# First token tile of a flow-matching step: three z blocks multiplied in float32 while the modulation columns arrive in pairs, modulation as columns with stationary weights

## The chip, the core and the metric

The kernel runs on one core of a Trainium2 chip. The metric is device time in microseconds (us) for one execution. Three runs of the kernel before gave 2206.56, 2209.3 and 2211.78 us (median 2209.3). One execution was recorded by the hardware profiler; its span, from the first to the last instruction, is 2205.0 us.

The engines are named as in the profile: PE multiplies matrices, PEld is its weight load (one operand of a product is loaded and stays put, "stationary", while the other "moves" through), DVE, ACT and POOL work on vectors, and SP issues most of the loads and stores.

## The reference, cut to what matters

One layer for two groups of tokens, 2048 sample tokens and 128 prompt tokens, each of 1024 numbers. Only the head of it is touched here:

```python
def ada_mod(cvec, w, b):
    m = jnp.einsum('...d,de->...e', jax.nn.silu(cvec), w) + b
    return jnp.split(m, 3, axis=-1)

shift, scale, gate = ada_mod(c, w_ada[l], b_ada[l])
xn = rmsnorm(h, ln_g[l]) * (1.0 + scale[:, None, :]) + shift[:, None, :]
...
proj = jnp.einsum('btd,de->bte', xn, w_in)
qkv, beta, dec, z_a, u_b, v_b, z_b, x_c, z_c, gates = jnp.split(proj, points, axis=-1)
...
o = rmsnorm(o, o_norm_g) * jax.nn.silu(z_a.astype(jnp.float32).reshape(B, T, H_A, DV))
```

So a vector product with `w_ada` (1024 x 2048 of it is used here, 8.4 MB) gives a shift and a scale for each of the 1024 channels, the normalised tokens are modulated with them, and then multiplied by the columns of `w_in`. The four blocks of 128 columns called z (`z_a`, silu of the product) come first.

## The kernel before, in words

**The shape of the work.** A channel index of 1024 is eight rows of 128 partitions, `k` = 0..7 (`KT` = 8). Tokens are cut into tiles `TBS`: four of 512 and one of 128. Products with `w_in` are made in three float16 parts: a weight block is split into `hi` and `lo`, the modulated tokens into `xh` and `xl`, and for each `k` there are three products, hi·xh, hi·xl, lo·xh (`gemm_T`, all recorded under L161, where the helper `mm` stands). To split without overflow, one scale `sx` for all tokens is taken from a bound on the modulation (L425 to L430).

**The modulation.** L396 to L415 run over eight blocks of 256 columns of `w_ada`; blocks 0 to 3 are shift, 4 to 7 are scale. Each block comes in two loads `ast` of 512 KB (L403, `ast` has 8 buffers). The products have the two condition columns `scT` stationary and the weights moving: eight products of 256 columns in float32 for a block. In blocks 0, 2, 4 and 6 (`AD`) the second half is instead summed on DVE (`ada_sum`, L384 and L386) and added through two products with `sel`. The result is a row, copied (L413) and turned into columns by small products with the identity (L415), all eight blocks into the one bank `pa`. The first token tile is loaded ahead of block 4 (`XB`).

**What follows it.** When the last block is in, L420 to L422 make `sh` and `ms` for all eight `k`, then come the bound and `sx`. Four z weights are fetched (`getw(4)` with two `wst` buffers, so that the third and fourth load when the first two have been split) and converted to `zhi` and `zlo` (L209, L222, L223).

**The tile loop** (L442 to L472) does for each of the five tiles: squares of the tokens on ACT (L451), the reciprocal root (L170 on DVE, L171 on POOL), scaling on DVE (L455), transposing on PE (L459; 128 x 128 pieces, 32 for a tile of 512), modulating into `xm` on DVE (L461), `xh` on ACT (L462), `xl` on POOL (L463), then four z blocks of 24 products, each with a sigmoid on ACT (L468), a gating product on DVE (L469) and a store (L471).

**What sets the order.** The program is written once, and a scheduler puts the instructions of each engine into one fixed sequence. An engine executes its own sequence in order: an instruction that waits holds up all behind it on that engine, loads on SP as well. A load into a buffer waits until the last reader of that buffer is done. Behind the tile loop the z results are used much later; the q, k and v blocks of `w_in` follow at once.

## Time and profile before

| what | value |
|---|---|
| three runs | 2206.56, 2209.3, 2211.78 us |
| span of the profiled execution | 2205.0 us |
| PE busy, share of the span | 2139.0 us, 97% |
| DVE, ACT, POOL busy | 1295.6, 1007.0, 704.9 us |
| granted PE clock, mean | 0.993 |
| first and last product of the tile loop on PE start at | 48.97 and 154.21 us |

The span is what the trace shows of the profiled execution; the median run is 4.3 us longer than it. PE is busy for 97% of the span, and most of what it isn't lies in the first 70 us, which is the part that the change rewrites. In the timeline a row is: start, duration, engine, line, operation, result <- operands, size, count, and in brackets the idle time before it with what ended it. In the table of windows each engine has its busy time in that stretch; PEclk is the granted PE clock, then come the busy share of the DMA engines and the rate in GB/s.

### The profile page before, as it was taken

To read this page: it belongs to the slowest core of one execution; us is meant where nothing else is said; L and a number is where in the kernel's file an instruction comes from. 1 tells how busy PE (TensorE), PEld (TensorE's weight loads), DVE (VectorE), ACT (ScalarE), POOL (GpSimd) and SP (SyncE) were. 2 spreads that over 40 slices of the span, in tenths; PEclk is the share of its full clock that TensorE was granted. 3 is DMA by queue.
4 is the path that set the end of the run, shared out by engine and by line. 5 is a ranking of instruction groups with operands and counts; after the bars stand their busy time and mean duration, and the time that the engine had idled before them with its cause. 6 is when DMAs were issued, how large, how long until landed. Compare 5 with 4: busy or idle time off the path is not lost. (4 is left out here: it accounts for less than half of the span.)

```text
span 2205.0 us, 42035 instructions
## 1 busy us (share of the span) xinstructions
PE 2139.0 (97%) x15966; PEld 1233.8 (56%) x15966; DVE 1295.6 (59%) x3081; ACT 1007.0 (46%) x2322; POOL 704.9 (32%) x860
## 2 busy tenths in 40 slices
PE   7999999999999999999999999999999999999998
PEld 3564444456555588878555555556554444444443
DVE  5736954479889778255665555765674544223454
ACT  3644744445465464344644445665553422222332
POOL 1421333223343322432322223354542221122543
PEclk9999999999999999999999999999999999999999
DMA  8434823177786662443665555776664544324542
GB/s 280 143 96 147 287 94 107 63 210 221 232 245 221 203 186 88 116 122 114 220 182 162 163 167 183 238 212 213 193 197 151 168 127 131 117 77 125 170 149 103
DMA packets 304276, 365.05 MB, mean 166 GB/s; under 512 B 39393, under 2 KB 215626, under 8 KB 302026
## 3 DMA queue, kind: packets, MB, share of 16 engines
q1 hardware_dynamic: 288938, 302.19, 45.5%
q0 software_dynamic: 12688, 51.27, 6.4%
q10 hardware_dynamic: 2448, 8.91, 1.0%
q8 instruction: 125, 2.05, 0.4%
q14 instruction: 77, 0.63, 0.1%
HBM read 234.67 MB, written 127.62 MB: 164 GB/s over the span
## 5 line engine op out<-in xcount | busy, mean ns | idle before, releaser
L161 PE MATMUL b<-xh,whi 128*128 128x512 f16 (+1 forms) x1920 | 650.4, 347 | 3.2 <-DVE mrow L1361 1.2
L161 PE MATMUL b<-xl,whi 128*128 128x512 f16 (+1 forms) x1920 | 650.9, 347 | 0.0
L161 PE MATMUL b<-xh,wlo 128*128 128x512 f16 (+1 forms) x1920 | 650.4, 347 | 0.0
L161 PEld LDWEIGHTS <-whi 128*128 128x128 f16 x3904 | 358.1, 98 | 328.8 <-issue 7.9
L161 PEld LDWEIGHTS <-wlo 128*128 128x128 f16 x1952 | 191.3, 98 | 179.8 <-issue 2.4
L161 PE MATMUL b<-big,bhi 128*128 128x512 f16 (+1 forms) x960 | 251.6, 348 | 2.2 <-ACT big L1325 1.5
L1365 POOL TENSOR_TENSOR mrow<-mrow,sg 128x512 f32<-128x512 f32 (+1 forms) x80 | 91.9, 1149 | 296.5 <-DVE sg L1364 216.3
L161 PE MATMUL b<-big,blo 128*128 128x512 f16 (+1 forms) x480 | 163.7, 348 | 0.0
L1355 ACT ACTIVATE sg<-b,winv 128x512 f32<-128x512 f32 (+1 forms) x120 | 74.2, 618 | 170.5 <-PE b L161 169.6
L161 PEld LDWEIGHTS <-xh 128*128 128x128 f16 x1496 | 117.6, 98 | 30.2 <-issue 1.5
L161 PEld LDWEIGHTS <-bhi 128*128 128x128 f16 x960 | 86.7, 98 | 73.1 <-issue 2.7
L1364 DVE SCALAR_TENSOR_TENSOR sg<-b,binv,sg 128x512 f32<-128x512 f32 (+1 forms) x80 | 53.4, 668 | 125.2 <-PE b L161 118.1
L632 POOL TENSOR_TENSOR cy<-cy,raw 128x545 f32<-128x545 f32 (+1 forms) x48 | 66.9, 1421 | 183.4 <-ACT raw L631 183.4
L175 DVE CAST wscb<-wss 128x1 bf16<-128x1 f32 x93 | 14.3, 154 | 154.7 <-ACT wlo L209 65.8
L852 POOL COPY T<-ES 32x256 f16<-32x256 f16 x68 | 32.3, 475 | 207.1 <-DMA ES<-ei 168.2
L161 PE MATMUL b<-wlo,xh 128*128 128x128 f16 x544 | 92.9, 219 | 0.0
L161 PE MATMUL b<-whi,xh 128*128 128x128 f16 x544 | 92.9, 219 | 0.0
L161 PE MATMUL b<-whi,xl 128*128 128x128 f16 x544 | 92.9, 219 | 0.0
L161 PE MATMUL b<-wohi,mh 128*128 128x512 f16 x240 | 90.9, 379 | 1.3 <-ACT mh L1432 1.3
L161 PE MATMUL b<-wohi,ml 128*128 128x512 f16 x240 | 90.8, 379 | 0.3 <-DVE ml L1433 0.3
L161 PE MATMUL b<-wolo,mh 128*128 128x512 f16 x240 | 90.9, 379 | 0.0
L223 DVE SCALAR_TENSOR_TENSOR wlo<-wst,wsc,whi 128x1024 f16<-128x1024 f32 x52 | 70.4, 1358 | 30.8 <-ACT whi L222 30.7
(449 smaller groups left out, 4284.0 us busy)
## 6 DMA issues: line engine op xcount, KB each, us to landing
wst<-in_w_in_dram SPq DMA_DIRECT2D x60, 512.0 KB
qkv<-cy POOLq DMA_DIRECT2D x12, 1089.0 KB, 5.3
st<-br SPq DMA_DIRECT2D x48, 256.0 KB
mrow<-mrg SPq DMA_DIRECT2D x18, 512.0 KB
mrow<-mrg SPq DMA_DIRECT2D x16, 576.0 KB
mrg<-mrow POOLq DMA_DIRECT2D x16, 576.0 KB, 3.6
...
```

The lines of the kernel that those rows point to most:

```text
L161: PE.matmul(out, l, r, start=start, stop=stop)
L175: V.tensor_copy(sb16, ss)
L223: V.scalar_tensor_tensor(w.lo, st, s, w.hi, ALU.mult, ALU.subtract)
L632: G.tensor_tensor(y[:, c0:c1], y[:, c0:c1], raw[:, 1 + c0:1 + c1], ALU.mult)
L852: G.tensor_copy(T16[rows(a0, b), :, :, b], ES[0:32, :, 2 * a0 + b, :, wT])
L1355: A.activation(sg, ps, AF.Sigmoid, scale=gw.inv)
L1364: V.scalar_tensor_tensor(sg, ps, binv[:, 1:2], sg, ALU.mult, ALU.mult)
L1365: G.tensor_tensor(mr, mr, sg, ALU.add)
```

## The change

The modulation is now made as columns: 128 x 128 pieces of `w_ada` are the stationary operand and the two columns of `scT` move, so each product gives 128 channels for both groups at once, and neither the row copy nor the transposes to columns are needed. The blocks are taken in pairs, `j` = 0..3: shift block `j` and scale block `4 + j`. For the pairs 1 to 3 both halves of the scale block are summed on DVE (16 instructions) and added by four products with a column of ones. After a pair, `sh` and `ms` of two `k` are known.

The first token tile is loaded at the very start, normalised and transposed into `xT` (`xT` takes the second of two token buffers). Each pair modulates two `k` of `xT` in place, and six float32 products of 512 columns follow, one for each of the two `k` and of three z blocks, which gather in three banks. The z weights 0 to 2 are loaded in float32 into `ast` buffers and stay in them until they are converted, after the last pair. The second token tile and the fourth z weight are loaded after the last `ada` block. `sx` comes after the last pair as before. During the z blocks of tile 1, `xh` and `xl` of tile 0 are made from `xT` (xl now on DVE); the fourth z block of tile 0 is done in float16 after tile 1. Tiles 1 to 4 are otherwise as before. The float16 products of three z blocks of tile 0 (3 x 24) are gone.

In the changed kernel the helper `mm` is at L159, the sums at L382 and L384, the loads at L395 (`w_ada`) and L400 (z), the modulation of `xT` at L457, the casts of tile 0 at L521 and L522.

```diff
-XB = 4
-AD = (0, 2, 4, 6)
...
-    for blk in range(8):
-        if blk == XB:
-            load_x(*TBS[0])
-            columns()
-        ps = bank(ps_d, [2, 256])
-        for k0 in range(0, KT, 4):
-            st = sb(p0p, [P, 4, 256], "ast", bufs=8)
-            last_ada = SY.dma_start(st, w_ada_[k0 * P:(k0 + 4) * P, blk * 256:(blk + 1) * 256].rearrange("(k p) c -> p k c", p=P))
-            if k0 and blk in AD:
-                acc = sb(p0p, [P, 2, 256], "aacc")
-                ada_sum(acc, st, range(k0, k0 + 4))
-                for g in range(2):
-                    mm(ps, sel[:, g, :], acc[:, g, :], False, g == 1)
-                continue
-            for k in range(4):
-                mm(ps, scT[:, k0 + k, :], st[:, k, :], k0 + k == 0, k0 + k == KT - 1)
-        adr = sb(p0p, [2, 256], "adr")
-        V.tensor_copy(adr, ps)
-        for k in range(2):
-            PE.transpose(pa[:, blk * 2 + k, :], adr[:, k * P:(k + 1) * P], ident[:2, :2])
...
-        V.tensor_tensor(sh, pa[:, 0:8, :], spread(49, 57), ALU.add)
-        V.tensor_tensor(ms, pa[:, 8:16, :], spread(57, 65), ALU.add)
-        V.scalar_tensor_tensor(ms, ms, 1.0, spread(0, 8), ALU.add, ALU.mult)
...
-        read_next()
-        read_next()
-        load_x(*TBS[1])
-        zaw = getw(4)
...
+    def read_ada(blk, k0):
+        st = sb(p0p, [P, 4, 256], "ast", bufs=8)
+        d_ = SY.dma_start(st, w_ada_[k0 * P:(k0 + 4) * P, blk * 256:(blk + 1) * 256].rearrange("(k p) c -> p k c", p=P))
+        return st, d_
+
+    def read_z(g):
+        st = sb(p0p, [P, KT, P], "ast", bufs=8)
+        SY.dma_start(st, w_in_[:, C_ZA + g * P:C_ZA + (g + 1) * P].rearrange("(k p) c -> p k c", p=P))
+        return st
+
+    load_x(*TBS[0])
+    columns()
+    ms = sb(cp, [P, KT, 2], "ms")
+    sh = sb(cp, [P, KT, 2], "sh")
+    T0 = TBS[0][1]
+    xT = sb(p0p, [P, KT, T0], "xt")
+    spread = lambda a, n: pc[:, a:a + n].rearrange("p (k o) -> p k o", o=1).to_broadcast([P, n, 2])
+    zst, zps = [], []
+    for j in range(4):
+        pa = bank(ps_x, [P, 2, 2, 2])
+        for s_, blk in enumerate((j, 4 + j)):
+            acc = sb(p0p, [P, 2, 256], "aacc") if j and s_ else None
+            for k0 in range(0, KT, 4):
+                st, last_ada = read_ada(blk, k0)
+                if acc is not None:
+                    ada_sum(acc, st, range(k0, k0 + 4), k0 == 0)
+                else:
+                    for c_ in range(2):
+                        for k in range(4):
+                            mm(pa[:, s_, c_, :], st[:, k, c_ * P:(c_ + 1) * P], scT[:, k0 + k, :], s_ + c_ + k0 + k == 0, j == 0 and s_ + c_ + k0 + k == KT + 1)
+            if acc is not None:
+                for c_ in range(2):
+                    for g in range(2):
+                        mm(pa[:, s_, c_, g:g + 1], acc[:, g, c_ * P:(c_ + 1) * P], ones[:, 0:1], False, c_ + g == 2)
+            if j == 0 and s_ == 0:
+                zst.append(read_z(0))
+        if j == 0:
+            zst.extend([read_z(1), read_z(2)])
+            xt = normed(*TBS[0])
+            for k in range(KT):
+                ps = bank(ps_d, [P, T0])
+                for i in range(4):
+                    PE.transpose(ps[:, i * P:(i + 1) * P], xt[:, i, k * P:(k + 1) * P], ident)
+                A.copy(xT[:, k, :], ps)
+            zps.extend(bank(ps_mm, [P, T0]) for _ in range(3))
+        kk = slice(2 * j, 2 * j + 2)
+        with tc.high_priority():
+            V.tensor_tensor(sh[:, kk, :], pa[:, 0], spread(49 + 2 * j, 2), ALU.add)
+            V.tensor_tensor(ms[:, kk, :], pa[:, 1], spread(57 + 2 * j, 2), ALU.add)
+            V.scalar_tensor_tensor(ms[:, kk, :], ms[:, kk, :], 1.0, spread(2 * j, 2), ALU.add, ALU.mult)
+            for k in (2 * j, 2 * j + 1):
+                V.tensor_scalar(xT[:, k, :], xT[:, k, :], ms[:, k, 0:1], sh[:, k, 0:1], ALU.mult, ALU.add)
+        for k in (2 * j, 2 * j + 1):
+            for g in range(3):
+                mm(zps[g], zst[g][:, k, :], xT[:, k, :], k == 0, k == KT - 1)
...
+        load_x(*TBS[1])
+        zst.append(read_z(3))
+        zaw = [convert(st, KT, tag="z") for st in zst]
+        wdone.extend(zaw)
+        wread.extend([None] * 4)
+        wnext[0] = 4
+        fetch(4)
...
+    def z_out(g, t0, ps, scale):
+        tn = ps.shape[-1]
+        sg = sb(ep, [P, tn], "sg", bufs=4)
+        A.activation(sg, ps, AF.Sigmoid, scale=scale)
+        V.scalar_tensor_tensor(sg, ps, scale, sg, ALU.mult, ALU.mult)
+        if szlate:
+            SY.dma_start(*szlate.pop())
+        szlate.append((szD[g, :, t0:t0 + tn], sg))
+
+    def z_unit(g, t0, tn):
+        ps = bank(ps_d if tn == P and g % 2 else ps_mm, [P, tn])
+        gemm_T(ps, zaw[g], 0, xh[:, :, t0:t0 + tn], xl[:, :, t0:t0 + tn])
+        z_out(g, t0, ps, zaw[g].inv)
+
+    for g in range(3):
+        z_out(g, 0, zps[g], 1.0)
+    for ti, (t0, tn) in enumerate(TBS):
+        if ti == 0:
+            continue
+        if t0 not in xts:
+            load_x(t0, tn)
+        g = 0 if t0 < NS else 1
+        nt = tn // P
+        xt = normed(t0, tn)
...
+            z_unit(g, t0, tn)
+            if ti == 1:
+                for k in (2 * g, 2 * g + 1):
+                    A.activation(xh[:, k, 0:T0], xT[:, k, :], AF.Copy, scale=sx)
+                    V.scalar_tensor_tensor(xl[:, k, 0:T0], xT[:, k, :], sx, xh[:, k, 0:T0], ALU.mult, ALU.subtract)
+        if ti == 1:
+            z_unit(3, 0, T0)
```

**The loads on SP, up to the second token tile (`xt_314` before, `xt_436` after).** Names: `ast` loads of 512 KB, `wst` two weights of later blocks, `st` a weight of a much later stage; "waits" names what must be done first, DMAHW a load, PE and DVE those engines. Before, from the ninth load of `w_ada`:

```order
L403 DMA ast_207<-in_w_ada_dram 128x4x256 [waits DMAHW1_49,PE_49]
L403 DMA ast_213<-in_w_ada_dram 128x4x256 [waits DMAHW2_49,DVE_49]
L403 DMA ast_231<-in_w_ada_dram 128x4x256 [waits DMAHW3_49,PE_49]
L637 DMA st_3946<-in_w_spatial_dram 128x4x128 [waits DMAHW4_49]
L403 DMA ast_237<-in_w_ada_dram 128x4x256 [waits DMAHW5_49,PE_49]
L403 DMA ast_248<-in_w_ada_dram 128x4x256 [waits DMAHW6_49,PE_49]
L403 DMA ast_254<-in_w_ada_dram 128x4x256 [waits DMAHW7_49,DVE_49]
L403 DMA ast_272<-in_w_ada_dram 128x4x256 [waits DMAHW0_49,PE_49]
L403 DMA ast_278<-in_w_ada_dram 128x4x256 [waits DMAHW1_49,PE_49]
L195 DMA wst_310<-in_w_in_dram 128x8x128 [waits DMAHW2_49]
L195 DMA wst_312<-in_w_in_dram 128x8x128 [waits DMAHW3_49]
L393 DMA xt_314<-in_x_sample_dram 128x4x1024 [waits DMAHW4_49]
```

After, from a load of pair 0 (`ast_249`) and the two for pair 1's scale block (`ast_270`, `ast_280`) on:

```order
L395 DMA ast_259<-in_w_ada_dram 128x4x256 [waits DMAHW4_49,PE_49]
L395 DMA ast_270<-in_w_ada_dram 128x4x256 [waits DMAHW5_49,PE_49]
L395 DMA ast_280<-in_w_ada_dram 128x4x256 [waits DMAHW6_49,PE_49]
L395 DMA ast_306<-in_w_ada_dram 128x4x256 [waits DMAHW7_49,PE_49]
L395 DMA ast_316<-in_w_ada_dram 128x4x256 [waits DMAHW5_49,DMAHW0_49,DVE_49]
L395 DMA ast_327<-in_w_ada_dram 128x4x256 [waits DMAHW6_49,DMAHW1_49,DVE_49]
L395 DMA ast_337<-in_w_ada_dram 128x4x256 [waits DMAHW2_49,PE_49]
L395 DMA ast_363<-in_w_ada_dram 128x4x256 [waits DMAHW3_49,DMAHW1_49,DVE_49]
L395 DMA ast_373<-in_w_ada_dram 128x4x256 [waits DMAHW4_49,PE_49]
L395 DMA ast_384<-in_w_ada_dram 128x4x256 [waits DMAHW7_49,PE_49]
L395 DMA ast_394<-in_w_ada_dram 128x4x256 [waits DMAHW2_49,DVE_49]
L390 DMA xt_436<-in_x_sample_dram 128x4x1024
```

In both, a load waits for the engine that last read its buffer. Now `ast_316` waits for the sums over `ast_270`, `ast_327` for those over `ast_280`, `ast_363` for those over `ast_327`, and `ast_394` for those over `ast_337`. Three of the eight buffers are held by z weights all the while.

**PE around the end of the modulation.** Before, from the last `w_ada` loads to the first z product (`b_113` is the bank `pa`, `b_421` and up are transposed tokens, `zhi_316` the first z weight):

```order
L161 MATMUL b_271<-ast_272,scT_105 2x256 x4
L415 MATMUL b_113<-cst_87,adr_243 128x2 x2
L459 MATMUL b_421<-cst_87,xt_196 128x128 x4
L161 MATMUL b_271<-ast_278,scT_105 2x256 x3
L161 MATMUL b_247<-aacc_256,sel_109 2x256 x2
L161 MATMUL b_271<-ast_278,scT_105 2x256
L415 MATMUL b_113<-cst_87,adr_267 128x2 x2
L459 MATMUL b_430<-cst_87,xt_196 128x128 x4
L415 MATMUL b_113<-cst_87,adr_284 128x2 x2
L459 MATMUL b_439<-cst_87,xt_196 128x128 x4
L161 LDWEIGHTS ones_2_89
L161 MATMUL b_298<-xscb_299,ones_2_89 128x1
```

After, from the transposes of tile 0 to the products of pair 1 (`b_248`, `b_305`, `b_362` are the modulation banks of pairs 1, 2 and 3; `b_234` to `b_236` the three z banks, `ast_147`, `ast_169`, `ast_171` the z weights):

```order
L159 MATMUL b_248<-scT_105,ast_259 128x2 x8
L159 MATMUL b_248<-cst_87,aacc_269 128x1 x4
L159 MATMUL b_305<-scT_105,ast_306 128x2 x8
L159 MATMUL b_305<-scT_105,ast_316 128x2 x8
L159 MATMUL b_362<-scT_105,ast_363 128x2 x5
L159 MATMUL b_305<-cst_87,aacc_326 128x1
L159 MATMUL b_362<-scT_105,ast_363 128x2
L159 MATMUL b_234<-xt_125,ast_147 128x512
L159 MATMUL b_235<-xt_125,ast_169 128x512
L159 MATMUL b_236<-xt_125,ast_171 128x512
L159 MATMUL b_234<-xt_125,ast_147 128x512
L159 MATMUL b_235<-xt_125,ast_169 128x512
```

Five products of pair 3's shift block (`ast_363`) stand ahead of the six z products of pair 1 (of which the first five are shown); the z products of pairs 2 and 3 come after the rest of pair 3's modulation.

**DVE at the last pair** (`rs_543` is the reciprocal root of tile 1, `xt_125` is `xT`, `xt_436` tile 1). After:

```order
L453 TENSOR_TENSOR sh_124<-b_305,pc_108 128x4
L454 TENSOR_TENSOR ms_123<-b_305,pc_108 128x4
L455 SCALAR_TENSOR_TENSOR ms_123<-ms_123,pc_108 128x4
L457 TENSOR_SCALAR xt_125<-xt_125,ms_123,sh_124 128x512 x2
L168 TENSOR_SCALAR rs_543<-xss_538 128x4
L453 TENSOR_TENSOR sh_124<-b_362,pc_108 128x4
L454 TENSOR_TENSOR ms_123<-b_362,pc_108 128x4
L455 SCALAR_TENSOR_TENSOR ms_123<-ms_123,pc_108 128x4
L457 TENSOR_SCALAR xt_125<-xt_125,ms_123,sh_124 128x512 x2
L466 TENSOR_TENSOR bss_420<-bss_420 128x1
L413 TENSOR_SCALAR xt_436<-xt_436,rs_543 128x1024 x4
L173 CAST xscb_425<-bss_420 128x1
```

In the list before no token tile's reciprocal root stands between the sums and `sh`; now tile 1's stands ahead of pair 3's `sh`, `ms` and the modulation of its two `k`.

30 lines of the change are left out of this document (11 added, 19 removed).

## The prediction

> **What bounds the kernel now.** I read the page first, then a table of windows.
>
> ```profile
> span 2205.0 us, 42035 instructions
> PE 2139.0 (97%) x15966; PEld 1233.8 (56%) x15966; DVE 1295.6 (59%) x3081; ACT 1007.0 (46%) x2322; POOL 704.9 (32%) x860
> ...
> 0.00:10.00 10.00, 2.54 (x7) 0.93 (x8) 0.95 (x4) 1.47 (x2) 0.62 (x9) 1.00 0.73 234
> 10.00:20.00 10.00, 10.00 (x45) 3.73 (x43) 5.93 (x16) 0.00 (x0) 0.00 (x0) 1.00 1.08 369
> 20.00:30.00 10.00, 8.14 (x33) 2.84 (x32) 4.59 (x13) 4.60 (x8) 1.18 (x1) 0.83 1.05 344
> 30.00:40.00 10.00, 9.11 (x46) 3.70 (x45) 5.88 (x14) 0.74 (x1) 0.00 (x0) 1.00 1.12 318
> 40.00:50.00 10.00, 6.11 (x34) 4.17 (x32) 6.50 (x29) 6.16 (x14) 1.23 (x1) 0.83 0.49 178
> 200.00:300.00 100.00, 100.00 (x558) 49.04 (x557) 79.89 (x74) 65.86 (x86) 37.11 (x38) 1.00 0.65 224
> ```
>
> PE is busy for all of 200 to 300, so whatever the start gives PE late, the end gets late: behind the tile loop both kernels issue the same PE sequence. The question is when the tile loop ends on PE. From 10 to 40 the loads run at 318 to 369 GB/s with a busy share above 1: the start is bound by loads, not by PE. The timeline shows the end of the loads, and the way to the first z product:
>
> ```profile
> 35.94 1.89 PE L161 MATMUL b<-ast,scT 128*2 128x256 f32 x8 [0.90 <-DMA ast<-in_w_ada_dram]
> ...
> 45.01 0.16 PE L161 MATMUL b<-xscb,ones 128*128 128x1 bf16 x1 [0.69 <-DVE xscb L175]
> ...
> 46.00 1.15 ACT L222 ACTIVATE zhi<-wst,wsc 128x1024 f16<-128x1024 f32 x1 [1.43 <-DVE wsc L186]
> ...
> 46.34 0.81 DVE L461 TENSOR_SCALAR xm<-b,ms,sh 128x512 f32<-128x512 f32 x1
> ...
> 48.09 0.60 ACT L462 CAST xh<-xm 128x512 f16<-128x512 f32 x1
> ...
> 48.97 0.63 PE L161 MATMUL b<-xh,zhi 128*128 128x512 f16 x1
> ...
> 154.21 0.22 PE L161 MATMUL b<-xh,zlo 128*128 128x128 f16 x1
> ...
> 154.27 0.38 PE L161 MATMUL b<-xh,whi 128*128 128x512 f16 x1
> ```
>
> PE last waits for a load of `w_ada` at 35.94; the bound's product runs at 45.01, the first z product at 48.97, the next stage starts at 154.27. So 105.3 us of tile loop follow 49 us of start. I work out both for the changed kernel.
>
> **What the change saves in the loop.**
>
> ```profile
> 65.86 0.38 PE L161 MATMUL b<-xl,zhi 128*128 128x512 f16 x1
> ...
> 70.40 0.38 PE L161 MATMUL b<-xl,zhi 128*128 128x512 f16 x1
> ...
> L459 PE MATMUL b<-cst,xt 128*128 128x128 f32 x117 | 17.0, 279 | 1.1 <-DVE wsc L186 0.9 <-issue 0.2
> ...
> 54.49 1.04 PE L459 MATMUL b<-cst,xt 128*128 128x128 f32 x8
> ```
>
> Between 65.86 and 70.40 lie 21 products back to back: 0.216 each. Three blocks of 24 go: 15.5. Of 117 transposes behind the first z product (this row is of the stretch 49 to 154.5) 80 stay behind it in the new order; 37 at (1.04 - 0.28)/7 = 0.109 make 4.0. The loop becomes 105.3 - 15.5 - 4.0 = **85.8**, if its other stalls (the few us of PE idle that windows after 50 show) stay as they are; I keep 2 either way. So the change breaks even if its first float16 z product starts at 154.3 - 85.8 = **68.5**, 19.5 later than now.
>
> **What it adds ahead of the loop: the loads up to pair 1.** In the new SP order, constants 0.4 MB, a token tile 2.1, six `ada` loads, three z weights, two weights of later blocks at 0.524 MB each, one of 0.26, and `ast_270` itself make 9.05 MB. The first 10 us carry 2.34 (234 GB/s); 6.71 at 344 GB/s take 19.5, so 29.5. I add 1 for landing (0 to 2.4, what a lone load below takes beyond its bytes) and 1 since z rows are 512 bytes, half of an `ada` row (an estimate; the window with such loads has 318 GB/s): **31.5** (30 to 33). The same rule without that last us puts the last `ada` of before (11.15 MB) at 36.6, and the trace has 35.94.
>
> **Waits in series.** Three z weights hold three of eight `ast` buffers, so `ast_327` is loaded only when the sums over `ast_270` and `ast_280` are done, and `ast_363` only after those over `ast_327`.
>
> ```profile
> 9.22 0.62 DVE L384 TENSOR_SCALAR aacc<-ast,scT 128x256 f32<-128x256 f32 x2 [4.45 <-DMA ast<-in_w_ada_dram]
> ...
> 9.75 2.46 DVE L386 SCALAR_TENSOR_TENSOR aacc<-ast,scT,aacc 128x256 f32<-128x256 f32 x6
> ...
> 49.92 2.60 SPq L195 DMA_DIRECT2D wst<-in_w_in_dram  x2
> ...
> 53.82 1.06 ACT L209 ACTIVATE zlo<-wst 128x1024 f16<-128x1024 f32 x1 [0.32 <-DMA wst<-in_w_in_dram]
> ...
> 1568.25 5.71 DMA wst<-in_w_in_dram
> 1617.40 3.94 DMA wst<-in_w_in_dram
> ```
>
> Eight sums take 12.21 - 9.22 = 3.0; sixteen take 0.53 + 14 x 0.40 + 0.1 = 6.2. A load of 512 KB that finds the queue nearly empty takes 3.9 from issue to its reader (49.92 to 53.82); the chain of waits has others of 3.94 and 5.71. So: 31.5 + 6.2 = 37.7, load 3.9: 41.6, eight sums: 44.6, load of `ast_363`: **48.5**. The bounds of a lone load are 2.4 (its bytes at 369 GB/s and 1 to land) and 5.7, so -3.0 to +3.6 for two. [...]
>
> PE can do nothing else then: five products with `ast_363` stand ahead of pair 1's six z products, though these have had their operands since about 48 (sh, ms and 2 modulated `k` behind the sums on DVE). PE idles from about 43, when the products with `ast_316` end.
>
> **PE from 48.5.**
>
> ```profile
> 31.21 3.62 PE L161 MATMUL b<-ast,scT 128*2 128x256 f32 x16
> ...
> 176.75 0.84 PE L161 MATMUL b<-tok,cst 128*128 128x68 f32 x6
> ...
> L161 PE MATMUL b<-tok,cst 128*128 128x68 f32 x4 | 0.6, 262 | 0.0
> ...
> 42.65 0.28 PE L415 MATMUL b<-cst,adr 2*128 2x2 f32 x2 [1.35 <-DVE adr L413]
> ...
> L415 PE MATMUL b<-cst,adr 2*128 2x2 f32 x16 | 2.1, 206 | 1.9 <-DVE adr L413 1.9
> ...
> 7.75 5.92 PE L161 MATMUL b<-ast,scT 128*2 128x256 f32 x16 [3.40 <-DMA ast<-in_w_ada_dram]
> ```
>
> A float32 product is two records; eight of 256 columns (16 records) keep (3.62 - 0.38)/15 = 0.216 a record, so 512 columns take 4 x 0.216 = 0.863. Eighteen are left (pairs 1 to 3): **15.5**. A small product (128 x 128 float32 stationary, two columns moving) is not in the trace. The nearest row is 128 x 68 moving with such a stationary operand: (0.84 - 0.26)/5 = 0.116 a record, 0.23 a product. The lower end is two 2 x 2 records in 0.28, one of them 0.21 by the mean of its group: 0.07 a record, 0.14; the upper is 0.43, a product at the cold spacing of the row at 7.75. In the order 24 stand among the z products: 24 x 0.23 = **5.5** (3.4 to 10.3).
>
> After its first wait PE ran 16 records in 5.92 instead of 3.62, and each of the two windows with an idle PE has clock 0.83, a loss of 10 x 0.17 = 1.7. PE idles 5 us before 48.5 and again before pair 3, so two such losses: **3.4** (1.7 to 6.8). The Trainium skill ("TensorE: Matmul & The Clock Gate", HAM oscillation) says that an idle gap beyond about 3.4 us brings half clock for about as long; the two windows at 0.83 agree, and by the page a shorter second wait would cost nothing: 1.7 less.
>
> Pair 3's modulation stands on DVE behind `rs_543`, tile 1's reciprocal root, which needs ACT's squares of tile 1, loaded last.
>
> ```profile
> 24.50 1.06 ACT L451 ACTIVATE jk<-xt 128x1024 f16<-128x1024 f32 x1
> 25.68 1.06 ACT L451 ACTIVATE jk<-xt 128x1024 f16<-128x1024 f32 x1
> ```
>
> Its load goes out when the sums over `ast_337` end (48), behind three `ada` loads: 1.57 + 2.10 MB at 344 GB/s from about 47 land at 57.7. Four squares at a pitch of 1.18 and two of weights that stand among them on ACT (1.06 each, the row at 53.82) end at 64.5; `sh` and `ms` (0.5) and the first modulated `k` (0.8, the row at 46.34) at 65.8. PE would be there at 48.5 + 5.5 + 12 x 0.863 + 1.7 = 66.1, so there may be no wait, or up to 2; I charge **0.5**. Sum: 48.5 + 5.5 + 15.5 + 3.4 + 0.5 = **73.4** for the last float32 z product.
>
> **From there to the first float16 product.** Before, 45.01 to 46.00 (0.99) from the bound's product to ACT's use of the scales, and 0.88 from the first cast's start to the product. Now the bound's product stands behind the z products on PE, one gated product (0.75) more on DVE in its chain, and on ACT the eight casts of tile 0 and a `zhi` ahead of tile 1's first cast:
>
> ```profile
> L469 DVE SCALAR_TENSOR_TENSOR sg<-b,winv,sg 128x512 f32<-128x512 f32 x16 | 11.7, 746 | 13.3 <-ACT sg L468 13.3
> ...
> L462 ACT CAST xh<-xm 128x512 f16<-128x512 f32 x31 | 18.7, 616 | 17.6 <-DVE xm L461 17.2
> ```
>
> A cast from SBUF with a scale is half of the 1024-wide square, 0.53, and at most the 0.62 of this row: 8 x 0.53 + 1.15 = 5.4. So 0.99 + 0.75 + 5.4 + 0.88 = 8.0: first float16 product at **81.4**, end of the loop at 81.4 + 85.8 = **167.2**, 12.9 later than 154.3. That is 32.4 us more start for 19.5 us less loop. What is removed from the start (the row copies, 2.1 us of transposes to columns, the wide products) lay beside loads and bounds nothing now. Against its own span of 2205.0 the sum is 2217.9; the median run is 4.3 longer, so **2222.2, forecast 2222**. About 0.2%, 4.4 us, is what a measurement can tell from no change.
>
> **Rivals.**
> *Half clock through the float32 products.* If the waits between pairs keep the clock down, 15.5 becomes 31 instead of 18.9: +12.1, 2234. The windows at 0.83 rather than 0.5 and the full spacing soon after 31 speak against it. 0.12.
>
> *A smaller slip: the buffers hold nothing up.* If the loads flow, the last `ada` lands at 10 + (13.77 - 2.34)/0.344 = 43.2, with landing 45; PE could do pair 1 and 2 by then, but `rs_543` still holds pair 3: tile 1 lands at 43.2 + 6.1 + 1 = 50.3, squares to 57.1, first modulated `k` 58.4, six products 63.6, +8.0 +85.8 = 157.4: +3.1, 2212. The waits for DVE on SP speak against it; half of the way there (one of the two lone loads falls away) is 2217. 0.08, half of it within 0.2%.
>
> *Faster: neither buffers nor tile 1's root hold the last pair.* Then 45 + 3.0 (sums) + 0.9 + 1.5 + 5.2 = 55.6, +8.0 +85.8 = 149.4: -5, 2204. The point from which it decides: the last float32 product must end by 68.5 - 8.0 = 60.5, so pair 3 be modulated by 55.3 rather than 65.8. Both orders are fixed sequences, so I give it 0.05.
>
> *No difference.* If every bounded cost fell at its low end (small products -2.1, clock -1.7, lone loads -3.0, loads ahead -1.5, wait -0.5, loop -2: -10.8), +2.1 would be left: 2211. Or the stores and weights behind the loop absorb the slip; PE's 100.00 in 200 to 300 speaks against it. 0.05.
>
> **How the numbers follow.** The forecast has 0.70, with 2216 to 2230 as its own range from the bounds (of opposite signs, not all at one end). The range 2213 to 2234 leaves out the faster case, most of the case of no difference, half of the smaller slip and about half of the half-clock one: 0.05 + 0.04 + 0.04 + 0.06 = 0.19. Slower by over 0.2% (above 2213.7): 0.70 + 0.12 + 0.04 = 0.86; same 0.05 + 0.04 = 0.09; faster 0.05.
>
> **What would show it.** Right: `ast_327` and `ast_363` issued when sums end, gaps of PE of some 5 us before `ast_363`, first float16 z product at 78 to 85, next stage at 163 to 172, the rest shifted alike. Wrong: a first float16 product before 70; loads issued without waits; PEclk at 0.5 from 48 to 74; a loop much shorter than 84 or, with ACT and DVE making tile 0's casts beside tile 1's, longer than 90.

## The result and the profile after

The changed kernel takes 2224.09 us (median of 6 runs, 2219.06 to 2230.25) against 2209.48 us for the kernel before in the same sessions (6 runs, 2206.56 to 2211.78): a ratio of 1.0072 with a 95% interval of 1.0056 to 1.0087, 12 to 19 us slower. The forecast was 2222. The span of the profiled execution is 2222.1 us, 17.1 more than before. The page and the table of windows (after each engine's busy time: granted PE clock, DMA share, GB/s):

```profile
span 2222.1 us, 42123 instructions
PE 2146.2 (97%) x15998; PEld 1252.4 (56%) x15998; DVE 1301.7 (59%) x3106; ACT 1010.8 (45%) x2330; POOL 696.7 (31%) x852
...
10.00:20.00 10.00, 6.25 (x29) 6.09 (x29) 1.49 (x5) 5.74 (x10) 1.02 (x1) 1.00 1.01 320
20.00:30.00 10.00, 10.00 (x49) 10.00 (x49) 2.76 (x8) 3.13 (x6) 0.00 (x0) 1.00 1.15 305
30.00:40.00 10.00, 10.00 (x56) 7.13 (x54) 6.77 (x18) 3.14 (x7) 0.00 (x0) 1.00 0.68 219
40.00:50.00 10.00, 7.12 (x53) 7.03 (x53) 6.61 (x20) 0.42 (x1) 0.00 (x0) 0.72 0.56 180
50.00:60.00 10.00, 9.64 (x24) 5.93 (x25) 6.64 (x18) 0.00 (x0) 0.00 (x0) 0.60 1.03 354
60.00:70.00 10.00, 10.00 (x46) 6.42 (x45) 2.41 (x11) 7.41 (x18) 0.57 (x1) 0.83 0.22 51
...
200.00:300.00 100.00, 99.82 (x556) 48.91 (x554) 77.68 (x71) 58.30 (x75) 31.64 (x27) 1.00 0.69 239
```

From 200 to 300 PE is as full as before, so most of the start's delay is carried on. But from 20 to 70 PE is idle for 3.2 us only, and its clock is at 0.60 to 0.83 from 40 to 70. The timeline of the start:

```profile
14.12 13.79 PE L159 MATMUL b<-scT,ast 128*128 128x2 f32 x64 [0.89 <-DMA ast<-in_w_ada_dram]
...
33.33 0.62 DVE L382 TENSOR_SCALAR aacc<-ast,scT 128x256 f32<-128x256 f32 x2 [2.41 <-DMA ast<-in_w_ada_dram]
...
39.59 1.84 PE L159 MATMUL b<-scT,ast 128*128 128x2 f32 x16
...
42.19 4.93 PE L159 MATMUL b<-scT,ast 128*128 128x2 f32 x32
43.39 0.62 DVE L382 TENSOR_SCALAR aacc<-ast,scT 128x256 f32<-128x256 f32 x2 [3.90 <-DMA ast<-in_w_ada_dram]
...
50.35 2.27 PE L159 MATMUL b<-scT,ast 128*128 128x2 f32 x10 [3.23 <-DVE xt L457]
...
53.34 7.75 PE L159 MATMUL b<-xt,ast 128*128 128x512 f32 x12
...
64.63 12.24 PE L159 MATMUL b<-xt,ast 128*128 128x512 f32 x24
...
69.18 0.17 DVE L168 TENSOR_SCALAR rs<-xss 128x4 f32<-128x4 f32 x1 [5.96 <-ACT jk L409]
...
76.82 0.17 PE L159 MATMUL b<-xscb,ones 128*128 128x1 bf16 x1
...
85.25 0.58 PE L159 MATMUL b<-xh,zhi 128*128 128x512 f16 x1 [2.89 <-ACT xh L515]
...
173.93 0.38 PE L159 MATMUL b<-xh,whi 128*128 128x512 f16 x1
```

These are the forecast's stations. The bound's product follows the last float32 z product at 76.8 (forecast 73.4), the first float16 z product comes at 85.25 (81.4; before 48.97), the next stage at 173.93 (167.2; before 154.27). So the stage is 19.7 us late; on the way to the end 2.6 are made up again.

In the next table the three stations are given for every run: start of the bound's product, of the first float16 z product, and of the next stage's first product on PE, each from the profiled execution, and the ratio of times to the kernel before with its interval.

| run | bound | first f16 | next stage | ratio |
|---|---|---|---|---|
| before | 45.0 | 49.0 | 154.3 | 1 |
| changed | 76.8 | 85.3 | 173.9 | 1.0072 (1.0056 to 1.0087) |
| e1 z weights in wst | 76.4 | 85.7 | 172.2 | 1.0079 (1.0058 to 1.0100) |
| e2 few float32 products | 69.5 | 83.6 | 170.6 | 1.0061 (1.0039 to 1.0083) |
| e3 columns alone | 58.8 | 62.0 | 166.5 | 1.0067 (1.0052 to 1.0083) |
| e4 rows, float32 tile 0 | 71.9 | 81.5 | 167.5 | 1.0073 (1.0057 to 1.0090) |
| e5 columns alone, wide products added | 70.4 | 73.6 | 178.1 | 1.0096 (1.0075 to 1.0117) |
| e6 as e4, few float32 products | 66.2 | 74.5 | 164.1 | 1.0029 (1.0017 to 1.0041) |
| e7 casts late | 76.3 | 80.1 | 173.3 | 1.0061 (1.0040 to 1.0081) |
| e8 rows, z in wst, casts late | 66.2 | 70.8 | 164.8 | 1.0051 (1.0033 to 1.0069) |
| e9 xT apart | 80.0 | 88.5 | 175.8 | 1.0058 (1.0035 to 1.0081) |
| e10 e8 and xT apart | 66.5 | 71.3 | 157.5 | 1.0008 (0.9995 to 1.0022) |
| e11 e10 with two float32 blocks | 63.0 | 66.9 | 163.2 | 1.0048 (1.0031 to 1.0066) |
| e12 e10 with columns | 77.8 | 82.8 | 168.3 | 1.0052 (1.0034 to 1.0070) |

The intervals are 5 to 9 us wide. A station is exact for its trace, but it stands for one execution. The changed kernel, e7 and e9 have the same sequence on PE, and on SP's queue, up to the bound's product, and yet it starts at 76.8, 76.3 and 80.0; by the spacing of the records the clock first comes up at 31, 37 and 38 us in them. So a difference of less than some 4 us between the stations of two runs is not put down to an edit, and larger ones are read together with the times. The trace of e4 is that of the fastest of its four executions (2215.14; median 2222.51).

### The profile page after: what moved, and what is told of

It reads as the page before. It is cut to its first block, busy times and chain, and to the rows that moved or that the text cites. A ratio compares the mean times of both kernels' runs of the same rounds, so it can differ in the third digit from the quotient of the medians.

```text
span 2222.1 us, 42123 instructions
## 1 busy us (share of the span) xinstructions
PE 2146.2 (97%) x15998; PEld 1252.4 (56%) x15998; DVE 1301.7 (59%) x3106; ACT 1010.8 (45%) x2330; POOL 696.7 (31%) x852
## 5 line engine op out<-in xcount | busy, mean ns | idle before, releaser
L159 PE MATMUL b<-xh,whi 128*128 128x512 f16 (+1 forms) x1920 | 649.3, 347 | 4.2 <-DVE vrow L1254 1.6
L159 PE MATMUL b<-xl,whi 128*128 128x512 f16 (+1 forms) x1920 | 649.8, 347 | 0.0
L159 PE MATMUL b<-xh,wlo 128*128 128x512 f16 (+1 forms) x1920 | 649.2, 347 | 0.2 <-DVE wlo L221 0.2
L159 PEld LDWEIGHTS <-whi 128*128 128x128 f16 x3904 | 357.0, 98 | 332.8 <-issue 12.1
L159 PEld LDWEIGHTS <-wlo 128*128 128x128 f16 x1952 | 190.8, 98 | 178.9 <-issue 0.7
L159 PE MATMUL b<-big,bhi 128*128 128x512 f16 (+1 forms) x960 | 250.4, 347 | 2.6 <-ACT big L1377 1.9
L159 PE MATMUL b<-big,blo 128*128 128x512 f16 (+1 forms) x480 | 163.0, 347 | 0.0
L159 PEld LDWEIGHTS <-xh 128*128 128x128 f16 x1496 | 117.6, 98 | 29.9 <-issue 1.2
L159 PEld LDWEIGHTS <-bhi 128*128 128x128 f16 x960 | 86.3, 98 | 74.1 <-issue 3.0
L684 POOL TENSOR_TENSOR cy<-cy,raw 128x545 f32<-128x545 f32 (+1 forms) x48 | 70.4, 1495 | 182.0 <-ACT raw L683 182.0
L159 PE MATMUL b<-wlo,xh 128*128 128x128 f16 x544 | 92.9, 219 | 0.0
L159 PE MATMUL b<-whi,xl 128*128 128x128 f16 x544 | 92.9, 219 | 0.0
L159 PE MATMUL b<-whi,xh 128*128 128x128 f16 x544 | 92.9, 219 | 0.0
L159 PE MATMUL b<-wohi,mh 128*128 128x512 f16 x240 | 90.9, 379 | 1.4 <-ACT mh L1484 1.4
L221 DVE SCALAR_TENSOR_TENSOR wlo<-wst,wsc,whi 128x1024 f16<-128x1024 f32 x52 | 72.2, 1390 | 32.4 <-ACT whi L220 32.2
L159 PE MATMUL b<-wohi,ml 128*128 128x512 f16 x240 | 90.8, 379 | 0.3 <-DVE ml L1485 0.3
L159 PE MATMUL b<-wolo,mh 128*128 128x512 f16 x240 | 90.9, 379 | 0.0
```

The costliest lines, as they stand in the source:

```text
L159: PE.matmul(out, l, r, start=start, stop=stop)
L221: V.scalar_tensor_tensor(w.lo, st, s, w.hi, ALU.mult, ALU.subtract)
L684: G.tensor_tensor(y[:, c0:c1], y[:, c0:c1], raw[:, 1 + c0:1 + c1], ALU.mult)
```

## The experiments

Three theories were set against each other. A: the `ast` buffers held by z weights and the sums on DVE put the loads in series, and that sets the last float32 product (the forecast's main story). B: PE's own work sets it. C, which came up on reading the trace of the changed kernel: the two-column products leave PE's clock at half, and that makes B worse.

**e1: fewer holds.** z weights 1 and 2 use the two `wst` buffers.

```diff
-        st = sb(p0p, [P, KT, P], "ast", bufs=8)
+        st = sb(wp, [P, KT, P], "wst", bufs=2) if g in (1, 2) else sb(p0p, [P, KT, P], "ast", bufs=8)
```

> The changed kernel, but z weights 1 and 2 are loaded into the two wst buffers (so the two weights of later blocks come later) and only z weight 0 holds an ast buffer. Theory A (buffer holds and the sums on DVE put the loads in series, and that sets the last float32 product): the load of pair 3's shift block no longer waits for two rounds of sums, lands some 8 us earlier, PE's gap of 3.2 us before it goes, the next stage starts at 167 to 170 instead of 173.9, the time falls by 4 to 7 us to 2217 to 2220. Theory B (PE's own work, float32 products and small products, sets it, the waits only move idle time): the loads come earlier but the last float32 product ends at 74 or later, the time falls by 0 to 3 us.

The loads came early, as meant: the last load of `w_ada` was issued at 43.1 instead of 50.7. The end hardly moved: the bound's product at 76.4 instead of 76.8, next stage 1.8 earlier, time unchanged within its interval. The windows of e1 say why:

```profile
40.00:50.00 10.00, 10.00 (x72) 8.80 (x71) 6.56 (x20) 1.07 (x2) 0.00 (x0) 0.92 0.83 253
50.00:60.00 10.00, 10.00 (x32) 5.99 (x33) 4.57 (x14) 4.11 (x9) 0.00 (x0) 0.74 0.51 177
60.00:70.00 10.00, 10.00 (x54) 7.18 (x53) 4.46 (x12) 2.29 (x8) 1.02 (x1) 0.94 0.00 0
```

With the waits gone PE is busy for every microsecond from 40 to 70. The gap of 3.2 us before 50.35 went into work that was queued anyway. A, as the only cause, fell. What the waits cost can't be read from one trace, though: in e1's the clock first comes up at 38 us (31 in the changed kernel). And in the traces of e7 and e9, which keep the waits, PE has no such gap, because its own work took that long. In e7 the products on both sides of it run on as one stretch:

```profile
45.04 7.22 PE L159 MATMUL b<-scT,ast 128*128 128x2 f32 x42
```

**e2: fewer float32 products.** k = 1 to 6 of the three z blocks are left out.

```diff
-        for k in (2 * j, 2 * j + 1):
+        for k in ((0,) if j == 0 else (KT - 1,) if j == 3 else ()):
             for g in range(3):
```

> The changed kernel without 18 of the 24 float32 products of tile 0 (k = 1 to 6 are left out, so three z blocks of tile 0 lack them); all loads, sums and modulations stay. Theory A (waits in series): PE only waits longer for pair 3's modulation, ready at 70; the last float32 product ends at 73 to 74 instead of 76.7, the time falls by 2 to 5 us. Theory B (PE's work): 18 x 0.863 = 15.5 us of work go, the time falls by 12 to 16 us to 2208 to 2212.

The bound's product comes 7.3 us earlier, but the first float16 product only 1.6 and the next stage 3.4, and the time can't be told from the changed kernel's. Between A and B at the first station, then, but the run doesn't part them cleanly: with the wide products gone the clock is at 0.53, 0.50 and 0.60 in the windows from 40 to 70, so that what is left takes longer. It also shows a second path: with PE out of the way, tile 1 (its squares end on ACT at 70, its scaled tokens on DVE at 74) and ACT's casts hold the first float16 product.

**e3: the columns alone**, on the kernel before.

```diff
-                for g in range(2):
-                    mm(ps, sel[:, g, :], acc[:, g, :], False, g == 1)
+                for c_ in range(2):
+                    for g in range(2):
+                        mm(pa[:, blk * 2 + c_, g:g + 1], acc[:, g, c_ * P:(c_ + 1) * P], ones[:, 0:1], False, False)
...
-            for k in range(4):
-                mm(ps, scT[:, k0 + k, :], st[:, k, :], k0 + k == 0, k0 + k == KT - 1)
-        adr = sb(p0p, [2, 256], "adr")
-        V.tensor_copy(adr, ps)
-        for k in range(2):
-            PE.transpose(pa[:, blk * 2 + k, :], adr[:, k * P:(k + 1) * P], ident[:2, :2])
+            for c_ in range(2):
+                for k in range(4):
+                    mm(pa[:, blk * 2 + c_, :], st[:, k, c_ * P:(c_ + 1) * P], scT[:, k0 + k, :], ...)
```

> The kernel before with one part of the change alone: the modulation as columns with the weights stationary (the same halves of blocks 0, 2, 4, 6 summed on DVE, added by four products with ones); order of loads and tile loop as before, all tiles in float16. If a small product costs 0.22 us as at full clock, 96 + 16 of them are 25 us beside loads of 36 us, and nothing changes: next stage at 153 to 156, time within 3 us of before. Theory C (small products leave the clock at half, 0.43 each): 48 us of PE work, more than the loads take, and the first z product comes 8 to 12 us later: next stage at 162 to 166, time up by 7 to 12 us.

Theory C, and a little beyond its numbers: first z product 13.1 us later, next stage 12.3. The group of the small products up to 62, and the last stretch of them with what follows:

```profile
L161 PE MATMUL b<-scT,ast 128*128 128x2 f32 x192 | 41.7, 352 | 3.2 <-DMA ast<-in_w_ada_dram 3.2
...
49.37 6.96 PE L161 MATMUL b<-scT,ast 128*128 128x2 f32 x32
...
62.03 0.63 PE L161 MATMUL b<-xh,zhi 128*128 128x512 f16 x1
```

192 records in 41.7 us are 0.217 each, twice the 0.106 of the changed kernel's stretch at 39.59 ((1.84 - 0.25)/15). From 7.6 to 56 PE does little but small products, with one gap of 0.6 us, and the spacing never changes: 48 us of PE work where the loads of before need 36. This part alone costs as much time as the whole change.

**e4: the other part alone.** Rows as before (scT stationary, 256 columns moving), all else as changed.

```diff
+            pr = bank(ps_d, [2, 256])
...
-                    for c_ in range(2):
-                        for k in range(4):
-                            mm(pa[:, s_, c_, :], st[:, k, c_ * P:(c_ + 1) * P], scT[:, k0 + k, :], ...)
+                    for k in range(4):
+                        mm(pr, scT[:, k0 + k, :], st[:, k, :], k0 + k == 0, k0 + k == KT - 1)
...
+            adr = sb(p0p, [2, 256], "adr", bufs=1)
+            V.tensor_copy(adr, pr)
+            for c_ in range(2):
+                PE.transpose(pa[:, s_, c_, :], adr[:, c_ * P:(c_ + 1) * P], ident[:2, :2])
```

> The changed kernel with the other part alone: tile 0 in float32 for three z blocks, pairs and loads as changed, but the modulation as before, scT stationary and 256 columns of weights moving, row copy and transposes to columns. Eight wide products at full clock cost what sixteen small ones do (3.5 us a block). Theory A: no difference beyond 2 us, for the loads and sums are the same. Theory C (small products let the clock fall, and 6 us of the start were lost to half clock after 30): the clock stays up through 44 to 58, the last float32 product ends 2 to 5 us earlier, the time falls by 2 to 5 us.

The clock stays at 1.00 in every window from 20 to 70. The bound's product is 4.9 us earlier, the next stage 6.4. The time does not show it (1.0073 beside 1.0072, each with an interval of 3 us and more either way); e10 and e12 show it. The other part, which is the float32 tile, the pairs and the order of loads together, thus also costs: the next stage is 13.2 us later than before.

**e5: wide products added to e3**, to see whether the small products' pace hangs on the clock. After each full block two float32 products of 512 columns of a constant go into a bank that nobody reads.

```diff
+    def warm(lm):
+        with tc.issue_after(lm.ins):
+            for _ in range(2):
+                mm(wb, ident, cst[:, 0:512])
```

> The columns alone (as in the run with only the columns), with work added: after each full block of small products two float32 products of 512 columns of a constant into a bank that nobody reads, 14 in all, 12 us at full clock. Theory C (the two-column products leave the clock at half, 0.213 us a record, and wide products in between bring it up): the small products fall to 0.11 a record, 25 us for all, and the last of them ends at 44 to 51 instead of 56, though 12 us of work were added; the first z product comes at 52 to 58 instead of 62. If 0.213 is what a load of weights with two columns behind it costs at any clock, the added work comes on top: last small product at 66 to 70, time up by another 8 to 12 us.

As a cure it failed: fourteen wide products don't keep the clock up, and the added work came on top (bound's product 70.4 instead of 58.8). In its stations the run thus came out as the rival said. The records decide against the rival all the same, since the same products stand in both clocks:

```profile
24.25 2.10 PE L161 MATMUL b<-scT,ast 128*128 128x2 f32 x16
26.21 1.03 PE L161 MATMUL b<-cst,aacc 128*128 128x1 f32 x8
27.11 2.70 PE L161 MATMUL b<-cst 128*128 128x512 f32 x4
29.60 3.63 PE L161 MATMUL b<-scT,ast 128*128 128x2 f32 x17
...
30.00:40.00 10.00, 10.00 (x37) 7.83 (x36) 5.26 (x12) 1.13 (x2) 0.00 (x0) 0.50 1.02 298
```

At 24.25 and 26.21, behind wide products, a small record takes 0.12 and 0.11; at 29.60, when the clock has dropped to the 0.50 of the window that follows, 0.21. So 0.21 is not the price of loading weights as such; it is that price at half clock.

**e6: e4 without the same 18 float32 products.** The edit is that of e2 on e4.

> The rows with float32 tile 0, without the same 18 of 24 float32 products (k = 1 to 6 of three z blocks of tile 0 are left out). Theory B (with the clock up, PE's work sets the end): the last float32 product ends 10 us or more before 71.9, the next stage starts at 155 to 158 instead of 167.5. Theory A (the last pair's modulation waits for loads, sums and tile 1's root, whatever PE does): 1 to 4 us earlier at the last float32 product, next stage at 162 to 167.

Bound's product 5.7 us earlier, next stage 3.4, of 15.5 us of work removed; the time fell clearly (1.0029 beside 1.0073 for e4, and the intervals don't meet). So PE's work counts. But the clock didn't stay up here: the windows from 40 to 70 have 0.83, 0.80 and 0.69, where e4 has 1.00. From 50 to 60 PE is busy for 3.8 us only, waiting for sums and modulations on DVE, and the last three float32 products take 5.4 us instead of 2.6. So behind PE's work stand the waits, neither theory is enough alone, and how much each has can't be read from this run.

**e7: tile 0's casts behind tile 1's** on ACT.

```diff
-            A.copy(xh[:, k, t0:t0 + tn], t)
+            lastc = A.copy(xh[:, k, t0:t0 + tn], t)
+            if k == KT - 1: castq[ti] = lastc
...
-                    A.activation(xh[:, k, 0:T0], xT[:, k, :], AF.Copy, scale=sx)
+                    with tc.issue_after(castq[1].ins):
+                        A.activation(xh[:, k, 0:T0], xT[:, k, :], AF.Copy, scale=sx)
```

> The changed kernel with the eight casts of tile 0 (xh, ACT) put behind tile 1's casts. If the way from the last float32 product to the first float16 one (8.5 us) is a term of the sum, all of its 4 to 5 us are saved: first float16 product at 80 to 81.5 instead of 85.25, next stage at 169 to 170, time down by 3 to 5 us. Rival: ACT, DVE and POOL have as much to do in the first 25 us of the loop either way, so what is saved ahead of the first product comes back as stalls behind it: first product earlier by 4, next stage within 1.5 of 173.9, time within 2 us of the changed kernel.

The rival was right at the stations: first float16 product 5.2 us earlier, next stage 0.7. What was won came back in the loop: PE is idle in it for 5.1 us (2.9 in the changed kernel), and the window from 105 to 115 has a clock of 0.82 (there 1.00). DVE and PE:

```profile
97.45 2.06 DVE L525 SCALAR_TENSOR_TENSOR xl<-xt,xsc,xh 128x512 f16<-128x512 f32 x3
...
100.89 1.28 DVE L221 SCALAR_TENSOR_TENSOR wlo<-wst,wsc,whi 128x1024 f16<-128x1024 f32 x1 [1.05 <-ACT whi L220]
102.10 0.74 DVE L489 SCALAR_TENSOR_TENSOR sg<-b,winv,sg 128x512 f32<-128x512 f32 x1
...
102.89 0.59 PE L159 MATMUL b<-xh,zhi 128*128 128x512 f16 x1 [3.27 <-DVE sg L489]
```

PE waits 3.3 us for a bank of z that DVE empties at 102.10, behind tile 0's low parts and a weight's, which stand there later than in the changed kernel. (This reads one trace; e9 and e10 try a part of it.)

**e8: three edits**, those of e4, e1 and e7.

> Three edits together on the changed kernel: rows instead of columns (scT stationary), z weights 1 and 2 in the wst buffers, casts of tile 0 behind tile 1's. If PE's clock, the buffer holds and the casts each cost what the sum gives them (clock 5, holds 4, casts 3), the last float32 product ends at 64 to 68, first float16 product at 70 to 73, next stage at 157 to 161, time 2210 to 2216: still 2 to 7 us slower than before. If only the clock matters, it is like the rows alone: next stage 165 to 168.

The start did what the sum said (bound's product 66.2, first float16 product 70.8). The loop did not: 164.8 - 70.8 = 94.0 us, where the changed kernel has 88.7, and so the next stage missed the 157 to 161 that were expected. (Some 2 us of the 94.0 are small products of the weight `bdp`, 32 records here and 3 in the changed kernel, most of which the other runs have behind this station.) PE in it, and the windows:

```profile
91.44 0.16 PE L159 MATMUL b<-wscb,ones 128*128 128x1 bf16 x1 [1.50 <-DVE wscb L173]
92.51 0.38 PE L159 MATMUL b<-xh,zhi 128*128 128x512 f16 x1 [0.91 <-DVE wsc L183]
...
106.93 0.16 PE L159 MATMUL b<-wscb,ones 128*128 128x1 bf16 x1 [2.58 <-DVE wscb L173]
```

```profile
85.00:105.00 20.00, 16.94 (x86) 8.40 (x85) 15.02 (x33) 16.50 (x29) 1.18 (x2) 1.00 0.77 252
105.00:115.00 10.00, 7.45 (x34) 4.49 (x34) 8.28 (x20) 7.53 (x12) 5.60 (x6) 0.83 0.07 28
```

PE is idle for 5.6 us of these 30, and its clock is at 0.83 in the second. Tile 2's load goes out at 78.73 only, so ACT has its squares between 87 and 96, among tile 0's casts and the weights' squares, and the weights' bounds (`wscb`) come late.

**e9: xT apart.** `xT` lies in a part of `xl` that is written later, so tile 2 has a buffer at once.

```diff
-    xT = sb(p0p, [P, KT, T0], "xt")
+    xT = xl[:, :, 1024:2048].bitcast(F32)
```

> The changed kernel, but xT lies in the space of tiles 2 and 3 of xl (not written before the casts of tile 0 are done), so the second token buffer is free and tile 2's load needs not wait for those casts. If the loop's stalls at 105 to 110 (2.5 us) come from tile 2's late load: that load is issued before 60 instead of 91, the stalls go, the loop is 86 to 87 us instead of 88.7 and the next stage starts at 170 to 172. Rival: DVE, ACT and POOL are what the loop waits for; then other stalls take their place and the next stage stays within 1 us of 173.9.

The load went out at 57.7 (90.78 in the changed kernel), PE is full from 105 to 115 (there 8.5 of 10), and the loop fell to 175.8 - 88.5 = 87.4, in which a wait of 3.5 us at 92 for POOL's low parts of tile 1 is left. But the start came 3.2 us later (by the spacing of its records the clock first came up at 38 instead of 31; the program up to there is the changed kernel's), so the next stage was 1.9 later instead of 2 to 4 earlier, the time the same. That the edit takes away the stall from 105 on is shown, a gain in the total is not.

**e10: e8 and xT apart.**

> Four edits together on the changed kernel: rows (clock up), z weights 1 and 2 in wst (fewer holds), casts of tile 0 behind tile 1's, xT in xl's space (tile 2 loads early). If the loop of 94 us in the run with the first three came from tile 2's late load, it falls to 86 to 89, with the first float16 product still at 70 to 72: next stage at 156 to 161, time 2209 to 2214, at most 3 us above before. If the loop is bound by the vector engines, it stays above 91 and the time within 3 us of the run with three edits (2217.5).

The loop is 157.5 - 71.3 = 86.2 us, 7.8 less than in e8, against the forecast's 85.8. PE waits in it for 2.3 us in all, for POOL's low parts of tile 1, and the clock is at 0.83 in the window from 70 to 80; from 80 on PE is full at 1.00. The longer of the two waits:

```profile
73.56 0.59 PE L159 MATMUL b<-xl,zhi 128*128 128x512 f16 x2 [1.26 <-POOL xl L521]
```

Of the 7.8 us some 2 are the products of `bdp`; the rest, less idle time (2.3 us instead of 6.2) and less time at half clock, hung on tile 2's buffer. The times bear it out: 1.0008 here, 1.0051 in e8, and the intervals don't meet. And the next stage starts 3.2 us behind that of the kernel before; the time is 1.0008 (0.9995 to 1.0022), no difference that can be measured. So these four account for nearly the whole loss.

**e11: e10 with two float32 blocks** (block 2 in float16 after tile 1, like block 3).

```diff
-            for g in range(3):
-                mm(zps[g], zst[g][:, k, :], xT[:, k, :], k == 0, k == KT - 1)
+            for g in range(2):
+                mm(zps[g], zst[g][:, k, :], xT[:, k, :], k == 0, k == KT - 1)
...
+            z_unit(2, 0, T0)
             z_unit(3, 0, T0)
```

> As the run with four edits, but two z blocks of tile 0 in float32 instead of three (block 2 is done in float16 after tile 1, like block 3). The theory that a float32 product of 0.863 us takes the place of three float16 products of 0.216 (0.648) and so pays only where PE would idle: 8 x 0.863 = 6.9 us less ahead of the loop, 5.2 us more in it, so 1 to 2 us better if PE is busy throughout the start, 0 to 5 us worse if it idles there anyway: first float16 product at 63 to 66, next stage within 3 us of the run with three blocks.

First float16 product 4.4 us earlier, of 6.9 us of work left out ahead of the loop; but the loop is 96.3 us, 10.1 more, and the next stage 5.7 us later, outside the 3 that were expected. 5.2 of the 10.1 are the 24 float16 products, and 2.4 are more idle time of PE (4.7 us instead of 2.3). Some more is a clock of 0.83 in the window from 90 to 100, where e10 has 1.00; the rest was not followed. The largest wait is one of PE for DVE ahead of a transpose:

```profile
86.45 6.09 DVE L529 SCALAR_TENSOR_TENSOR xl<-xl,xsc,xh 128x512 f16<-128x512 f32 x5
...
93.50 1.12 PE L517 MATMUL b<-cst,xt 128*128 128x128 f32 x4 [3.23 <-DVE wsc L184]
```

The copies that empty the transposes' banks stand on DVE behind the 6 us of tile 0's low parts. So two blocks don't pay in this form; whether they would without that wait was not tried.

**e12: e10 with the columns.**

> As the run with four edits, but with the columns of the change (128 x 128 weights stationary, two columns moving): three edits alone (z weights in wst, casts late, xT apart). Theory C (the columns' clock is what the rows cured): clock 0.5 for 10 us and more before 66, last float32 product at 73 to 80 instead of 66, next stage at 163 to 170 instead of 157.5, time 6 to 12 us above the run with four edits (2216 to 2223). Rival (with the other three cured the start has room enough for slow small products): next stage within 3 us of 157.5.

Theory C: 77.8, 82.8, 168.3, so 10.8 us later at the next stage than with rows, and the loop is the same (85.4). The windows from 40 of e10 and then of e12:

```profile
40.00:50.00 10.00, 8.67 (x37) 3.49 (x35) 10.00 (x30) 0.77 (x1) 0.00 (x0) 1.00 1.04 333
50.00:60.00 10.00, 9.80 (x30) 4.03 (x28) 5.57 (x14) 8.25 (x17) 1.02 (x1) 1.00 0.55 208
```

```profile
40.00:50.00 10.00, 10.00 (x59) 8.97 (x60) 6.25 (x19) 0.00 (x0) 0.00 (x0) 0.70 0.86 292
50.00:60.00 10.00, 10.00 (x27) 4.85 (x26) 4.34 (x15) 4.72 (x9) 1.02 (x1) 0.79 0.98 340
```

With rows the clock is 1.00 and PE has idle time left; with columns PE is full from 40 to 60 at a clock of 0.7 to 0.8. The times show the difference too (1.0052 against 1.0008, and the intervals don't meet). But not all of it is the pace of the small products. In e12's sequence the scaling of tile 2 (L413) stands on DVE ahead of pair 3's `sh`, in e10's behind it, and PE waits for pair 3's tokens:

```profile
67.16 2.74 DVE L413 TENSOR_SCALAR xt<-xt,rs 128x1024 f32<-128x1024 f32 x4 [1.19 <-POOL rs L169]
69.81 0.15 DVE L453 TENSOR_TENSOR sh<-b,pc 128x4 f32<-128x4 f32 x1
...
70.87 1.76 PE L159 MATMUL b<-xl,ast 128*128 128x512 f32 x2 [3.48 <-DVE xl L457]
```

With this wait of 3.5 us and the half clock behind it (0.83 from 70 to 80, 1.7 us) taken off, some 6 of the 11.3 us at the bound's product are left for the small products' pace. That is an estimate; no run parts the two.

## Why the prediction was right, point by point

**Direction and size.** Forecast 2222, measured 2224.09, and the mechanism "more start than the loop gives back, carried to the end by a full PE" holds: start 36.3 us longer (forecast 32.4), loop 16.6 shorter (forecast 19.5). That the total came within 2 us is partly luck: the next stage is 19.7 us late where 12.9 were forecast, and 5.1 of these 6.8 us of error had gone by the time the medians are compared (14.6).

**Loads ahead, 31.5.** `ast_270` was there at 33.3. The rate was taken too high: 344 GB/s against 320 and 305 in the windows from 10 to 30. 1.8 us short, just past the end of its range.

**Series of waits.** The terms are right: sums from 33.33, the next load in use at 43.39 (10.06; forecast 6.2 + 3.9), `ast_363` in use at 50.35 (7.0; forecast 6.9). The trace ends PE's gap before 50.35 with the modulation on DVE, which the products that follow don't read; what they read is `ast_363`, issued at 46.40, so the wait is taken to be that load's. But as a cause it was overrated. PE's gap was 3.2 us, not some 5, it is missing in e7 and e9, and e1 took the waits away without a gain in the time. The step that failed is that PE "idles from about 43": with the clock at half until 31 and again from 44 its work took until 47.1, and was a second chain of nearly the same length. The rival that the buffers hold nothing up priced that at some 10 us less; it left PE's own work at full clock.

**Small products and the clock.** 0.23 at full clock is about right (0.21), and so is the upper end of 0.43. The choice between them was wrong for most of the start: the clock was charged as two losses of 1.7, as if only idle time lowered it. It was at half until 31, from 44 to 58 and from 65 to 68 (from the 0.72, 0.60 and 0.83 of the windows, 2.8 + 4.0 + 1.7 = 8.5 us were lost between 40 and 70). The sum got away with it because some of that lay beside the waits: from 50.35 on 5.6 us were lost where it has 3.4, and the way from there to the bound's product took 26.5 us (forecast 24.9). The rival of half clock through the float32 products came true in part: the eighteen took 19.7 us (53.34 to 60.92 and 64.63 to 76.71), 4.2 above full clock, where that rival has 15.5. e12 against e10 gives the price of the columns with the other three edits in place: 10.8 us, the wait for tile 2's scaling among them. The sentence that what is removed from the start "bounds nothing now" was right of the kernel before, but what was put in its place, at half clock, does bound it: e3.

On this the Trainium skill ("TensorE: Matmul & The Clock Gate", Part 1) says that some 3.4 us of sustained activity bring the full clock, and that idle windows of that length take it away. The length shows here: each window at 0.83 has 3.4 us at half clock (0.17 x 10 x 2). The idle windows don't: in the kernel before PE's longest wait is 0.71 us in the window from 20 to 30 and 1.62 in that from 40 to 50, so the prediction's "the two windows at 0.83 agree" is right for the length alone. And sustained activity was not enough: in e3 PE was busy for 48 us almost without a gap and the clock did not come up. In these traces being busy with small products does not count as activity.

**Last float32 product to first float16 one, 8.0.** Measured 85.25 - 76.8 = 8.4. e7 shows that it is no price of its own, though: 5.2 us of it can be saved and 4.5 come back in the loop.

**Loop, 85.8.** Measured 88.7. The cut by 24 x 3 products and 37 transposes is right (80 transposes are left). Of the 2.9 beyond, less than one is idle time: PE is idle in the loop for 2.9 us, but it was for 2.2 before, and these are in the 85.8. The larger part is the clock. PE waits for 1.2 and 2.9 us ahead of the first float16 product, and from 82 to 92 the clock is at half. Inside the loop PE is busy for 5.5 us of that time, which costs 2.8; before, the half clock from 46.6 to 50 reached only 1 us into the loop and cost 0.5. The sum had no term for the clock in the loop. The windows from 85, and the timeline (PE, SP's queue, ACT):

```profile
85.00:105.00 20.00, 18.32 (x77) 8.04 (x77) 17.15 (x36) 12.81 (x21) 11.96 (x8) 0.82 0.58 211
105.00:115.00 10.00, 8.48 (x44) 4.05 (x42) 8.57 (x18) 9.62 (x19) 3.05 (x3) 1.00 0.38 126
```

```profile
87.10 0.58 PE L159 MATMUL b<-xl,zhi 128*128 128x512 f16 x1 [1.26 <-POOL xl L516]
...
90.78 5.59 SPq L390 DMA_DIRECT2D xt<-in_x_sample_dram  x2
...
98.91 1.06 ACT L409 ACTIVATE jk<-xt 128x1024 f16<-128x1024 f32 x1 [1.45 <-DMA xt<-in_x_sample_dram]
...
107.42 2.49 PE L512 MATMUL b<-cst,xt 128*128 128x128 f32 x12 [1.08 <-issue]
```

The first wait of PE is for tile 1's low parts; the second stands ahead of tile 2's transposes, whose load took the buffer of `xT`, went out at 90.78 (before: 55.56) and kept ACT waiting at 98.91. e9 takes that one away. In e1, e2 and e4 the buffer is the same, but the load goes out 1.8 to 1.9 us behind the first float16 product instead of 5.5, and PE has no wait there (loops of 86.0 to 86.9 us). The steps spoke of that buffer nowhere; the range had 2 for the loop.

**Carried to the end.** 19.7 us at the next stage, 17.1 at the end of the span, 14.6 between the medians. Where the 5 us were made up was not followed. Of the 66 us in which PE isn't busy in the kernel before, 16.3 lie in the first 70, which is not most of them; 44.5 lie behind 600, where part of a delay can vanish.

**Not settled.** How much of e4's 13.2 us is PE's float32 work and how much the loads' series (in e6 the clock fell as well); how the four edits of e10 share the loss, since rows against columns (e12) and `xT` apart (e8) are each worth some 9 to 10 us with the other three in place, and all four only 14 together; and whether fewer float32 blocks would pay without e11's stall.
